# One Strassen pair less in a weight-gradient matmul: 23 instead of 24, with a new order of visits and of the sums between them

## Chip, core and metric

The kernel runs on one core of a Trainium2 chip. The metric is device time in microseconds (us) of one execution. A profiled execution also gives a span: from the first to the last of the program's own instructions.

## What is computed

```python
batch, m, k, n = 16, 512, 1024, 768
input:       (16, 512, 1024) float32
grad_output: (16, 512, 768)  float32
grad_weight = np.einsum('bmk,bmn->kn', input, grad_output).astype(np.float32)
```

Batch and m are summed over together: with X the input as 8192 x 1024 and G the gradient as 8192 x 768, the result is X transposed times G, 1024 x 768.

## The kernel before

**Loads.** The 8192 rows are taken in 32 *pairs* of 256 rows, numbered 0 to 31 here as in `u` of the code. GpSimd's queue loads each of them with a cast from float32 to bfloat16: first G of the pair (line 113), then X (line 114). Only pairs 0 and 1 come in smaller pieces, and the first 128 rows of X and the first of G come in float32 over the queues of ScalarE and SyncE and are rounded on the chip (lines 88 to 91 and 210 to 220). Eight loads can be under way: in the built program each load from the ninth on waits for the one eight places before it, and from the buffers' second use on also for who used the buffer last. 14 pairs of buffers hold the loaded pairs (`PAIRS_HELD`), 9 the sums made from them (`SUMS_HELD`).

**Two kinds of pair.** `LOADS` (line 12) has one letter per pair. A *plain* pair ("s") is two items of 128 rows. X has a left and a right half of 512 columns, G two halves of 384. Each item is multiplied in four blocks A, B, C, D (half of X by half of G), and each block in four parts q of 128 columns of X: 16 matmuls an item, 32 a pair, each of a 128 x 128 weight and 384 columns. A *Strassen* pair ("P") takes its 256 rows as a 2 x 2 block product and forms it with seven products instead of eight: A, D and five more called m, n, o, p, q, each again in four parts: 28 matmuls a pair. For that VectorE makes five sums per pair (`sum_g1`, `sum_g2`, `sum_x1`, `sum_x2`, `sum_x3`, lines 132 to 157): `sum_g1` is the one addition that gives all three block sums of G, because G's column halves are swapped (`LEFT`, `RIGHT`), and `sum_g2` and `sum_x3` work in place. The products o and p need, besides the loaded X, only `sum_g2`; q and n need `sum_x1`; m needs `sum_x2`; A and D need `sum_x3`.

**Visits.** Nine running results A, B, C, D, m, n, o, p, q lie in SBUF in float32 (`acc`, `macc`). PSUM has eight banks, so two of the nine can be open at a time, four banks each: two *slots*. `ORDER` (lines 18 to 32) is written out by hand or by a search; each word is a *visit*. In `1p12:3~!0,0,1,0` the letter is the result, 12 says up to which of its items it goes, and `!` says that the visit closes the slot. To close is to bring the four banks back: by VectorE, which adds the bank to the running result (line 357), or by ScalarE. The number after the colon says for how many banks (the last ones) ScalarE does it: it copies the running result into the bank before the first matmul (`carry`, line 296), TensorE adds on top, and ScalarE copies the bank back (line 353). `^` and `~` let ScalarE fill those banks as soon as the slot's last user has left them, bank by bank (`^`) or when all four have been left (`~`). The digit in front (1 here) says how many entries of the *filler* list VectorE works off before the visit, and the four after `!` how many before each bank is closed. The filler list is the five sums of each Strassen pair in order and then the 20 `SHARES`, which add the five products to A, B, C and D at the end. `A36:0-q` opens A with ScalarE filling its banks with minus q (line 323).

So every engine's order is fixed: TensorE's by `ORDER`; VectorE's and ScalarE's by the closes and fills in it; GpSimd's by the pairs. A matmul waits for its pair to have landed, for the sums that it reads, and for its bank. The last visit is D; its last part is split in two (lines 388 to 402), so that the last stores are short.

Of the kernel before, what the change touches and what calls it, by code (L numbers as in the profile page):

```python
# [8 lines left out]

P = 128  # L10

LOADS = "ssssssPPPPPPPPPPPPPPPPPPPPPPPPss"

ORDER = (
    "A1:4!0,0,0,0 C1:3 B1:2 B2!0,0,0,0 C2!0,0,0,0 A2!0,0,0,0 D3:1 C3:2~ D4!0,0,0,0 C4!0,0,0,0 A4 "
    "B4:2~ A6!0,0,0,0 B6!0,0,0,0 D6!0,0,0,0 C8:3~!0,0,0,0 A8:4~!0,0,0,0 D8:1^!0,0,0,0 B10!0,0,0,0 "  # L20
    "C9 A10:3^!0,0,0,0 C12!0,0,0,1 B12:1~!0,0,0,2 D12:1~ 2A12:4 A13!0,1,2,2 D13 p2:4!0,0,0,0 "
    "n2:3!0,0,1,0 D14!0,0,0,0 m2:4!0,0,1,0 o3:4!3,0,0,0 1A15:1^!0,0,0,4 q3:4 q4!1,0,0,0 1p4:3~ "
    "n4:2!0,0,0,0 p5!1,0,1,0 2m4:2~ D17:2!0,0,0,1 o6:2!1,1,1,0 m6!1,0,0,0 A18:4~!1,0,0,0 4n6:2~ "
    "1n7!0,0,0,0 q7:2~!0,0,0,1 o8!0,1,0,0 3p8:2^ D19:4^ D20!1,1,0,1 p9!0,0,0,0 m9 2A21:4!0,0,3,0 "
    "m10!0,0,0,0 4q9:2~ 2n10:4!0,0,0,0 q11!0,0,3,0 o11:2~ 1p12:3~!0,0,1,0 o12!0,0,0,0 "
    "D24:1~!0,0,4,0 2A24:2~ A25!0,0,0,1 1m13:3^!0,0,0,0 n14!0,1,0,0 q14:4~!0,1,1,4 o15:2~ "
    "1D26:3~!0,2,0,0 o16!0,0,0,1 1m16!1,0,1,0 p16:4^ q17:3^!0,0,0,0 4p17!0,1,0,0 1n17 "
    "1A30:4!0,0,0,0 n18 4n19!1,0,0,1 D30:4^ o18:3~ 2D31!0,1,2,0 o20!1,1,1,0 2m20 m21!0,0,0,0 "
    "q21:3^!2,1,0,3 p19:4^ p20 A32:1^ A34!0,0,0,0 p21 4D34:3~!0,3,0,0 p23 p24!0,0,1,0 "
    "q24:2^!0,0,1,0 m24:3~!0,0,1,1 o24:3~!0,0,1,0 2n22:4~ 1n23 2A36:0-q n24!0,1,0,0 A39 "  # L30
    "B16:4!0,3,1,0 2A40!0,0,0,0 C16:3!0,0,1,1 D40!0,1,1,0 "
).split()


SHARES = (
    "t20 t21 t22 t23 l20 t10 t11 t12 l21 t13 l10 l11 l12 l13 l22 l23 l30 l31 l32 l33 "
).split()

WARMUP = [512] * 10 + [128] * 2
# [7 lines left out]
def kernel(  # L47
# [58 lines left out]
    xg = []  # L106
    for u, kind in enumerate(LOADS):
        pool = pairs if u else head
# [343 lines left out]
```

## Time and profile before

| | |
|---|---|
| median of 3 runs | 164.74 us (164.50 to 164.87) |
| the profiled execution | 164.74 us, its span 163.0 us |
| TensorE clock granted | 1.00 throughout |
| matmuls | 946: 12 of warm-up, 922 of 384 columns, 12 in the split last part |
| ScalarE copies bank to result / result to bank | 154 / 129 (4 of them minus q) |
| VectorE banks closed (the split one counted once) | 118 |
| VectorE sums / shares | 120 / 20 |

All times below that carry no other name are us from the start of the span of this one execution. Lines like L337 are lines of the kernel before. In a timeline row the first number is the start, the second the length from the first start to the last end of the merged instructions, `xN` how many they are, and the bracket how long the engine sat idle before them and what released it. TensorE's matmuls overlap: each row shows one as 0.33 us long, and the next starts before it ends.

### The profile page before, as it was taken

To read this page: it belongs to the slowest core of one execution; us is meant where nothing else is said; L and a number is where in the kernel's file an instruction comes from. 1 tells how busy PE (TensorE), PEld (TensorE's weight loads), DVE (VectorE), ACT (ScalarE), POOL (GpSimd) and SP (SyncE) were. 2 spreads that over 40 slices of the span, in tenths; PEclk is the share of its full clock that TensorE was granted. 3 is DMA by queue.
4 is the path that set the end of the run, shared out by engine and by line. 5 is a ranking of instruction groups with operands and counts; after the bars stand their busy time and mean duration, and the time that the engine had idled before them with its cause. 6 is when DMAs were issued, how large, how long until landed. Compare 5 with 4: busy or idle time off the path is not lost.

```text
span 163.0 us, 2787 instructions
## 1 busy us (share of the span) xinstructions
PE 156.8 (96%) x946; PEld 92.0 (56%) x946; DVE 140.2 (86%) x266; ACT 122.0 (75%) x289; POOL 34.8 (21%) x69
## 2 busy tenths in 40 slices
PE   8899969999999999999999999999999999999992
PEld 3365536666555556666566666555666655655661
DVE  0475845699898999999999999999798979999992
ACT  3875377655988999969987788689767659998830
POOL 7442222212222222222222222122222000000000
PEclk9999999999999999999999999999999999999999
DMA  5999999999999999999999999999999999600595
GB/s 174 297 211 213 215 210 214 214 215 212 212 213 212 213 211 216 212 212 212 213 215 213 214 213 214 214 212 212 210 214 215 211 211 215 135 4 2 197 367 208
DMA packets 12398, 33.40 MB, mean 205 GB/s; under 512 B 1376, under 2 KB 4192, under 8 KB 12384
## 3 DMA queue, kind: packets, MB, share of 16 engines
q0 software_dynamic: 9360, 28.64, 88.8%
q1 hardware_dynamic: 2592, 3.47, 6.1%
q10 hardware_dynamic: 432, 1.11, 1.8%
q8 instruction: 7, 0.11, 0.3%
q14 instruction: 7, 0.06, 0.1%
HBM read 58.72 MB, written 3.15 MB: 380 GB/s over the span
## 4 chain that ended last, share of the span: by engine, by line
PE 67%; DVE 14%; DMA 13%; ACT 2%; issue 2%; DVEq 0%; ACTq 0%; POOLq 0%
PE bank L337 66%; DMA xp<-in_input_dram 9%; DMA gp<-in_grad_output_dram 4%; DVE macc L357 3%; DVE ge L138 2%; DVE xe L148 2%; DVE gp L143 2%; DVE acc L357 2%; DVE xp L157 2%; ACT bank L296 1%; ACT macc L353 1%; DVE xe L152 1%; PE bank L392 0%; DVE acc L400 0%; DVEq L357 0%
## 5 line engine op out<-in xcount | busy, mean ns | idle before, releaser
L337 PEld LDWEIGHTS <-xp 128*128 128x128 bf16 x634 | 61.6, 98 | 44.9 <-DMA xp<-in_input_dram 2.0
L337 PE MATMUL bank<-gp,xp 128*128 128x384 bf16 x444 | 76.8, 326 | 2.1 <-DMA xp<-in_input_dram 1.4
L353 ACT COPY acc<-bank 128x384 f32<-128x384 f32 x71 | 31.1, 491 | 17.4 <-PE bank L337 17.0
L337 PEld LDWEIGHTS <-xe 128*128 128x128 bf16 x288 | 27.9, 98 | 19.5 <-DVE xe L148 0.5
L353 ACT COPY macc<-bank 128x384 f32<-128x384 f32 x83 | 35.4, 503 | 2.5 <-PE bank L337 2.4
L357 DVE TENSOR_TENSOR acc<-bank,acc 128x384 f32<-128x384 f32 x58 | 29.4, 552 | 9.0 <-PE bank L337 8.4
L296 ACT COPY bank<-macc 128x384 f32<-128x384 f32 x64 | 29.4, 501 | 6.7 <-DVE macc L357 4.4
L337 PE MATMUL bank<-ge,xp 128*128 128x384 bf16 x190 | 34.1, 326 | 0.1
L337 PE MATMUL bank<-gp,xe 128*128 128x384 bf16 x192 | 33.7, 326 | 0.0
L296 ACT COPY bank<-acc 128x384 f32<-128x384 f32 x61 | 27.5, 497 | 4.6 <-DVE acc L357 4.2
L357 DVE TENSOR_TENSOR macc<-bank,macc 128x384 f32<-128x384 f32 x52 | 26.5, 552 | 2.0 <-PE bank L337 2.0
L114 POOL DMA_DIRECT2D xp<-in_input_dram x30 | 16.0, 532 | 54.0 <-DMA xp<-in_input_dram 28.1
L113 POOL DMA_DIRECT2D gp<-in_grad_output_dram x30 | 16.0, 533 | 36.3 <-PE bank L337 13.5
L138 DVE TENSOR_TENSOR ge<-gp 128x1152 bf16<-128x1152 bf16 x24 | 18.1, 753 | 0.0
L337 PE MATMUL bank<-ge,xe 128*128 128x384 bf16 x96 | 17.3, 326 | 0.1
L157 DVE TENSOR_TENSOR xp<-xp 128x1024 bf16<-128x1024 bf16 x24 | 16.5, 687 | 0.0
L148 DVE TENSOR_TENSOR xe<-xp 128x1024 bf16<-128x1024 bf16 x24 | 16.4, 685 | 0.0
L194 DVE TENSOR_TENSOR acc<-acc,macc 128x768 f32<-128x768 f32 (+1 forms) x20 | 16.3, 873 | 0.0
L143 DVE TENSOR_TENSOR gp<-gp 128x768 bf16<-128x768 bf16 x24 | 13.3, 555 | 0.5
L152 DVE TENSOR_TENSOR xe<-xp 128x512 bf16<-128x512 bf16 x24 | 10.1, 420 | 0.0
L211 DVE CAST gp<-gf 128x192 bf16<-128x192 f32 (+1 forms) x2 | 0.6, 310 | 5.1 <-DMA gf<-in_grad_output_dram 5.1
L96 PE MATMUL bank<-const-bfloat16-1.0 128*128 128x512 bf16 (+1 forms) x12 | 3.9, 499 | 0.8 <-PEq L436 0.8
(18 smaller groups left out, 17.5 us busy)
## 6 DMA issues: line engine op xcount, KB each, us to landing
xp<-in_input_dram POOLq DMA_DIRECT2D x30, 512.0 KB, 16.8
gp<-in_grad_output_dram POOLq DMA_DIRECT2D x30, 384.0 KB, 16.7
out_dram<-acc SPq DMA_DIRECT2D x15, 192.0 KB, 2.0
xf<-in_input_dram ACTq DMA_DIRECT2D x2, 512.0 KB, 5.0
gp<-in_grad_output_dram POOLq DMA_DIRECT2D x3, 192.0 KB, 6.5
xp<-in_input_dram POOLq DMA_DIRECT2D x2, 256.0 KB, 7.8
gf<-in_grad_output_dram SPq DMA_DIRECT2D x2, 192.0 KB, 4.3
out_dram<-acc SPq DMA_DIRECT2D x1, 128.0 KB, 1.8
```

Of the source, the lines that this page charges most:

```text
L113: nc.gpsimd.dma_start(out=gp, in_=G[rows, :].rearrange("(p m) n -> p m n", m=2))
L114: nc.gpsimd.dma_start(out=xp, in_=X[rows, :].rearrange("(p m) k -> p m k", m=2))
L138: nc.vector.tensor_add(out=ge.rearrange("p a n -> p (a n)"), in0=g[:, 0 : 3 * NH], in1=g[:, NH : 4 * NH])
L143: nc.vector.tensor_sub(out=g[:, 0::3, :], in0=g[:, 0::3, :], in1=g[:, 2:0:-1, :])
L148: nc.vector.tensor_add(out=xe[:, 0:2, :].rearrange("p a k -> p (a k)"), in0=xp[:, 0, :], in1=xp[:, 1, :])
L152: nc.vector.tensor_add(out=extra[i][0][:, 2, :], in0=xp[:, 0, 0:KH], in1=xp[:, 1, KH:K])
L157: nc.vector.tensor_sub(out=x[:, 1:3, :], in0=x[:, 1:3, :], in1=x[:, 0::3, :])
L194: op(out=dst, in0=dst, in1=src)
L296: nc.scalar.copy(out=bank, in_=sum_of(p, q))
L337: nc.tensor.matmul(bank, stat, mov, start=opening and j == 0 and not carried, stop=close and j == len(items_now) - 1, skip_group_check=car ...
L353: nc.scalar.copy(out=dst, in_=bank)
L357: nc.vector.tensor_add(out=dst, in0=bank, in1=dst)
```

## The change

Three lists change and nothing else; every function stays as it is, the one addition for G's block sums and the early fills by ScalarE included.

```diff
-LOADS = "ssssssPPPPPPPPPPPPPPPPPPPPPPPPss"
+LOADS = "sssssssPPPPPPPPPPPPPPPPPPPPPPPss"
...
-    "A1:4!0,0,0,0 C1:3 B1:2 B2!0,0,0,0 C2!0,0,0,0 A2!0,0,0,0 D3:1 C3:2~ D4!0,0,0,0 C4!0,0,0,0 A4 "
-    "B4:2~ A6!0,0,0,0 B6!0,0,0,0 D6!0,0,0,0 C8:3~!0,0,0,0 A8:4~!0,0,0,0 D8:1^!0,0,0,0 B10!0,0,0,0 "
-    "C9 A10:3^!0,0,0,0 C12!0,0,0,1 B12:1~!0,0,0,2 D12:1~ 2A12:4 A13!0,1,2,2 D13 p2:4!0,0,0,0 "
-    "n2:3!0,0,1,0 D14!0,0,0,0 m2:4!0,0,1,0 o3:4!3,0,0,0 1A15:1^!0,0,0,4 q3:4 q4!1,0,0,0 1p4:3~ "
...
-    "D24:1~!0,0,4,0 2A24:2~ A25!0,0,0,1 1m13:3^!0,0,0,0 n14!0,1,0,0 q14:4~!0,1,1,4 o15:2~ "
-    "1D26:3~!0,2,0,0 o16!0,0,0,1 1m16!1,0,1,0 p16:4^ q17:3^!0,0,0,0 4p17!0,1,0,0 1n17 "
...
-    "q24:2^!0,0,1,0 m24:3~!0,0,1,1 o24:3~!0,0,1,0 2n22:4~ 1n23 2A36:0-q n24!0,1,0,0 A39 "
-    "B16:4!0,3,1,0 2A40!0,0,0,0 C16:3!0,0,1,1 D40!0,1,1,0 "
+    "A1:3!0,0,0,0 C1:1 B1:3 B2!0,0,0,0 C2!0,0,0,0 D2:3 A2 D3 A3 D4!0,0,0,0 A4 B4:1^!0,0,0,0 C4 "
+    "C6!0,0,0,0 A6!0,0,0,0 D6:2~!0,0,0,0 B6:3^ C8!0,0,0,0 B8!0,0,0,0 D8:2~!0,0,0,0 A8!0,0,0,0 "
+    "D9:2 B10!0,0,0,0 D10!0,0,0,0 A10 B12:2^!0,0,0,0 A12!0,0,0,0 D12:3 B14!0,0,0,0 D14!0,0,0,0 "
+    "C13:3^ C14!6,0,0,0 A15:1 1o2:4!1,1,1,0 q2:4!0,1,0,1 A16!0,0,0,0 D16:1^ p3:4!2,1,1,0 "
...
+    "2A28:2~!2,0,0,1 q13!0,0,0,0 n15:3~!2,0,1,1 D28:1^!0,0,1,0 o16:2^!0,0,0,0 q16:2~!2,0,0,1 "
+    "m15:3~ 1p17:3^!4,0,1,1 D30!1,0,0,0 m16 m18!0,0,0,0 q18:4~!1,1,0,1 A32 1n19:4^!4,0,1,2 "
+    "o20:1~!0,1,0,0 D34:3^ 4D35!1,0,0,0 A35!1,0,0,0 o22:2^ p21:4 5p23!1,0,1,1 o23!0,0,0,0 q21:2~ "
+    "q23!3,0,0,0 m21:4~ m23!2,1,0,0 n21:4~ A38:0-q n23!5,0,0,1 A40 B18:4!2,1,0,1 A41!0,0,0,0 "
+    "C17:3 C18!1,0,0,0 D41!3,0,0,0 "
...
-    "t20 t21 t22 t23 l20 t10 t11 t12 l21 t13 l10 l11 l12 l13 l22 l23 l30 l31 l32 l33 "
+    "l20 l21 l22 t20 t21 t22 t10 t11 t12 t13 l23 t23 l10 l11 l12 l13 l30 l31 l32 l33 "
```

Pair 6 becomes a plain pair. Read off the lists and the built program:

| | before | after |
|---|---|---|
| plain / Strassen pairs | 8 / 24 | 9 / 23 |
| matmuls of 384 columns, the split part counted as six | 928 | 932 |
| sums on VectorE | 120 | 115 |
| banks closed by VectorE / by ScalarE | 118 / 154 | 124 / 148 |
| banks filled by ScalarE (minus q among them) | 129 | 124 |
| shares, loads, stores | 20, 69, 17 | 20, 69, 17 |

The loads stand in the same order with the same sizes on the same queue.

## The prediction

> **What bounds the kernel now.** First the page's busy times and TensorE's timeline, to see whether its matmuls run back to back.
>
> ```profile
> PE 156.8 (96%) x946; PEld 92.0 (56%) x946; DVE 140.2 (86%) x266; ACT 122.0 (75%) x289; POOL 34.8 (21%) x69
> ```
> ```profile
> 5.18 15.42 PE L337 MATMUL bank<-gp,xp 128*128 128x384 bf16 x90 [0.50 <-DVE xp L211]
> 21.97 16.75 PE L337 MATMUL bank<-gp,xp 128*128 128x384 bf16 x102 [1.37 <-DMA xp<-in_input_dram]
> ...
> 140.62 2.76 PE L337 MATMUL bank<-gp,xp 128*128 128x384 bf16 x16
> 143.22 2.76 PE L337 MATMUL bank<-gp,xe 128*128 128x384 bf16 x16
> ...
> 147.88 7.96 PE L337 MATMUL bank<-gp,xp 128*128 128x384 bf16 x48
> ```
>
> Sixteen matmuls take 143.22 - 140.62 = 2.60 us: 0.1625 us each, the price of a matmul below. I call *delay* the start of the n-th matmul of L337 (from 0) less n x 0.1625. It only grows, and each step in it is a wait. Start: 5.18. Matmul 89 starts one length (0.33) before the first row ends: 20.60 - 0.33 - 14.46 = 5.81. Matmul 90: 21.97 - 14.63 = 7.34. In the row at 147.88 begins matmul 856 (72 follow of 928): 147.88 - 139.10 = 8.78. From there to the end it stays. So TensorE is paced by its own matmuls, 928 x 0.1625 = 150.8, plus three portions of waiting: 0.63 at the start, 1.53 in one piece before matmul 90, and 1.44 in small pieces from there to 147.88.
>
> Second, what the 1.53 waits for: GpSimd's timeline. Each load waits for the one eight places before it, so in this stretch its start tells when that one had landed.
>
> ```profile
> 16.44 0.53 POOL L114 DMA_DIRECT2D xp<-in_input_dram  x1 [1.91 <-DMA xp<-in_input_dram]
> ...
> 22.21 0.53 POOL L114 DMA_DIRECT2D xp<-in_input_dram  x1 [3.38 <-DMA xp<-in_input_dram]
> ...
> 25.90 0.53 POOL L114 DMA_DIRECT2D xp<-in_input_dram  x1 [1.93 <-DMA xp<-in_input_dram]
> ...
> 30.21 0.53 POOL L114 DMA_DIRECT2D xp<-in_input_dram  x1 [1.91 <-DMA xp<-in_input_dram]
> ...
> 34.52 0.53 POOL L114 DMA_DIRECT2D xp<-in_input_dram  x1 [1.93 <-DMA xp<-in_input_dram]
> ```
>
> These are X of pairs 2 to 6 landing: 16.4, at most 22.2 (TensorE goes on at 21.97, so by then), 25.9, 30.2, 34.5. Pair 3 is 1.4 late against the pace of 4.32 a pair. I put pair u at 25.9 + 4.32 x (u - 4).
>
> Third, the small pieces: busy times by stretch, and VectorE at 98 us.
>
> ```profile
> 38.00:102.32 64.32, 64.14 (x392) 37.71 (x390) 62.64 (x122) 55.15 (x134) 15.90 (x30) 1.00 1.07 213
> ```
> ```profile
> 97.50 0.56 DVE L143 TENSOR_TENSOR gp<-gp 128x768 bf16<-128x768 bf16 x1
> 97.97 0.68 DVE L148 TENSOR_TENSOR xe<-xp 128x1024 bf16<-128x1024 bf16 x1
> 98.58 0.42 DVE L152 TENSOR_TENSOR xe<-xp 128x512 bf16<-128x512 bf16 x1
> 98.91 0.69 DVE L157 TENSOR_TENSOR xp<-xp 128x1024 bf16<-128x1024 bf16 x1
> 99.51 0.75 DVE L138 TENSOR_TENSOR ge<-gp 128x1152 bf16<-128x1152 bf16 x1
> 100.30 0.56 DVE L143 TENSOR_TENSOR gp<-gp 128x768 bf16<-128x768 bf16 x1
> ...
> 102.17 1.02 DVE L357 TENSOR_TENSOR macc<-bank,macc 128x384 f32<-128x384 f32 x2
> ```
>
> VectorE (third busy time) works 62.64 of 64.32, as tight as TensorE: whenever a sum or a close stands late in its queue, TensorE waits a tenth or a quarter of a us. From start to start a pair's five sums cost 0.47 + 0.61 + 0.33 + 0.60 + 0.79 = 2.80, and a bank 1.02 - 0.55 = 0.47. On ScalarE four copies back to back took 1.63 us at 5.55 and seven fills 2.96 us at 19.66: (1.63 - 0.48) / 3 = 0.38 and (2.96 - 0.48) / 6 = 0.41.
>
> **The change, part by part.** The sum is made against the span, 163.0; the profiled execution took 164.74, 1.74 more, and the median of the runs is the same 164.74.
>
> *Four matmuls more*: 4 x 0.1625 = **+0.65**, on TensorE's own path, nothing hides it.
>
> *VectorE*: five sums less, 2.80, and six banks more, 6 x 0.47 = 2.82: **0** in all. But it moves. By matmul 592 of the new order the queue holds 77 sums and 90 banks, by matmul 588 of the old one 83 and 90. Six sums, some 3.3 us, come later against the matmuls. If that room is not usable, the cover of the small waits stays as it is.
>
> *ScalarE*: six copies and five fills less, 6 x 0.38 + 5 x 0.41 = 4.3 us. ScalarE is busy 55.15 of 64.32 in the tight stretch, so this shortens no path by itself: **0**, hidden under TensorE.
>
> *The start.* The first 20 matmuls are the same ones; A1 now gives its first bank to VectorE, ahead of the rounding of G's right half: at most 0.1, covered by C1's four matmuls. The new order does B6 (eight matmuls on pair 2) before C8, so pair 3 is first read by matmul 96, not 90. If the delay stays at 5.81, TensorE is there at 5.81 + 15.60 = 21.41, pair 3 at 21.97: the wait shrinks from 1.53 to 0.56, and the delay after it is 21.97 - 15.60 = 6.37 instead of 7.34: **-0.97**. Cover: the fills of B6 and the closes of C6, A6 and D6 must be done by then; at 0.47 and 0.41 apiece they end near 21.0, with half a us in hand. Bounds: -0.97 and 0.
>
> *The next loads* must not take it back. With the delay at 6.37, first reads and landings are: pair 4, matmul 128, 27.2 against 25.9; pair 5, 152, 31.1 against 30.2; pair 6, 176, 35.0 against 34.5; pair 8, 229, 43.6 against 43.2; pair 13, 362, 65.2 against 64.8; pair 22, 602, 104.2 against 103.7; pair 28, 761, 130.0 against 129.6; pair 29, 785, 133.9 against 133.9. All in time, several by only 0.4. Where it fails, TensorE waits, and all later loads have that much more room. Most products also need sums after the landing. The tightest is q on pair 12 (matmul 341, 61.8), which needs `sum_x1`. From pair 10's landing at 51.8 VectorE's queue up to it holds 1.53 of pair 10's sums, 2.80 of pair 11's, 1.26 of pair 12's and seven banks, 3.29: 8.9 us, and it idles some 0.6 for o4's first bank: it comes to `sum_x1` at 61.3 and ends (0.68) at 62.0: 0.2 late.
>
> *The small waits*, 1.44 before, become s. At least 0.2 (pair 12); at most what they were, 1.44, unless something new turns up. VectorE has less in front of it, ScalarE 4.3 us less to do, which speaks for less; the landings are closer, which speaks against. I take **0.8**, the middle, since neither row decides.
>
> *The shares' order, the stores, GpSimd's loads*: the same instructions; the shares stand under the last 100 matmuls, where they stood, the last visit is D with 24 matmuls on a free slot as before, and the stores on SyncE's queue follow the same closes: **0**. If VectorE came late into D41 (three shares stand before its first bank, 1.4 us), the next banks cover it, 0.97 of matmuls for each 0.47.
>
> Sum: 163.0 + 0.65 - 0.97 - 1.44 + 0.8 = 162.04; with 1.74, **163.8**.
>
> [...]
>
> **The rivals.**
>
> *The landings take it back.* For: six of these first reads have 0.5 us or less in hand, and pair 3 shows that a load can be 1.4 late. Against: the other rows keep the pace within 0.05. One later load behind by pair 3's 1.4, with 0.4 in hand, gives 1.0 of wait; with 0.4 of the small waits left beside it s is 1.4: 164.4, at the edge of no change.
>
> *The head doesn't arrive.* The fills of B6 hold TensorE past 21.97, price up to the 0.97: 164.75, no change. For: fills and closes alternate on ScalarE there. Against: half a us in hand.
>
> *Sums in front of the only free slot: slower.* In the new order several sums stand in one heap before a bank that TensorE needs next: four before p17's first bank plus one before the visit, and D30 opens on p17's banks, because m15 holds the other slot. VectorE then has 2.80 + 0.47 = 3.3 us against p17's 2.6 us of matmuls: 0.7 late. The same heaps stand at C14 (6), n19 (5), p23 (6), n23 (5). Every heap at 0.6 makes 3.0 for five: s = 3.0, 166.0. It decides from s = 2.1 (0.65 - 0.97 - 1.44 + s above 0.33, the 0.2% that the measurement can tell). Against: VectorE comes to p17 with fewer sums behind it, and most heaps stand before long visits on the other slot.
>
> **How the numbers follow.** Forecast, s from 0.2 to 1.3, 163.2 to 164.3: 0.62. Landings: 0.14, half of it faster. Head: 0.09, no change. Heaps: 0.15, from 165.1 up. Below 164.41 (0.2% under 164.74): 0.62 + 0.07 = 0.69; within 0.2%: 0.07 + 0.09 = 0.16; slower 0.15. The range goes from 163.2, the forecast's own low end, over landings and head to 164.9.
>
> **What would show it.** In TensorE's timeline after: the run before pair 3 holds 96 matmuls, with an idle of about 0.4 before 21.97; the delay at the last visit is 6.9 to 7.7 instead of 8.78; no idle of over 0.6 after 22 us; 932 matmuls; VectorE's busy time within 1 us of 140.2 and ScalarE's 4 to 6 lower. Wrong would be: a delay above 7.3 at matmul 96, waits of TensorE for X after 22 us that add to over 1, or idle of 0.5 before D30, n19 or p23.

## The result and the profile after

| | before | after |
|---|---|---|
| median | 164.62 us (164.49 to 164.87, 4 runs) | 163.30 us (163.14 to 163.50, 4 runs) |
| span of the profiled execution | 163.0 us | 161.5 us |
| matmuls of 384 columns, the split part as six | 928 | 932 |

The ratio is 0.9918, 95% interval 0.9901 to 0.9936: 1.3 us faster, where 163.8 had been forecast. First the page of the kernel after: busy times, and the head of its chain of waits.

```profile
PE 157.4 (97%) x950; PEld 92.8 (57%) x950; DVE 140.9 (87%) x267; ACT 118.0 (73%) x278; POOL 34.8 (22%) x69
...
PE 84%; DMA 12%; issue 1%; DVE 0%; POOLq 0%
```

The head of the same chain in the kernel before:

```profile
PE 67%; DVE 14%; DMA 13%; ACT 2%; issue 2%; DVEq 0%; ACTq 0%; POOLq 0%
```

VectorE is where it was (140.2 before), ScalarE has 4.0 us less. VectorE and ScalarE, with 14% and 2% of the chain before, have all but gone from it. Next TensorE's timeline of the kernel after: start, length, engine, line, and in the bracket, if any, the idle time.

```profile
5.21 36.66 PE L337 MATMUL bank<-gp,xp 128*128 128x384 bf16 x218
...
146.97 7.35 PE L337 MATMUL bank<-gp,xp 128*128 128x384 bf16 x44
```

The long row of before broke after 90 matmuls, at the wait for pair 3. Here it runs on through 218. There is still a wait in it, too short to break a row in which each matmul counts as 0.33 us: matmul 95 starts at 21.31 and matmul 96, the first to read pair 3, at 21.73, 0.42 later instead of 0.1625. The delays (start of the n-th matmul less n x 0.1625) add it up:

| portion of the delay | before | after | change |
|---|---|---|---|
| up to and with the wait for pair 3 | 7.34 (matmul 90) | 6.13 (matmul 96) | -1.21 |
| small waits from there to the end | 8.78 - 7.34 = 1.44 | 6.61 - 6.13 = 0.48 | -0.96 |
| four matmuls more | | 4 x 0.1625 | +0.65 |
| sum | | | -1.52, the spans (163.0 and 161.5) say -1.5 |

GpSimd's timeline of the kernel after, X of pairs 2, 3 and 4 landing (each load starts when the one eight places before it is in):

```profile
16.45 0.53 POOL L114 DMA_DIRECT2D xp<-in_input_dram  x1 [1.93 <-DMA xp<-in_input_dram]
...
21.97 0.53 POOL L114 DMA_DIRECT2D xp<-in_input_dram  x1 [3.13 <-DMA xp<-in_input_dram]
...
25.95 0.53 POOL L114 DMA_DIRECT2D xp<-in_input_dram  x1 [1.93 <-DMA xp<-in_input_dram]
```

Pair 3 is late here too, by 0.24 less than before. The stretch of the small waits, in the columns us, PE, weight loads, VectorE, ScalarE, GpSimd, granted clock, DMA share, GB/s:

```profile
38.00:102.32 64.32, 64.32 (x396) 38.51 (x395) 61.86 (x119) 55.40 (x133) 15.90 (x30) 1.00 1.07 213
```

TensorE has no idle left and passes 396 matmuls instead of 392; VectorE works 0.78 us less in the same stretch (61.86 for 62.64). That work came earlier: between 21.97 and 38 us VectorE is busy 13.84 us instead of 10.74.

### The profile page after: what moved, and what is told of

It reads as the page before. It is cut to its first block, busy times and chain, and to the rows that moved or that the text cites. A ratio compares the mean times of both kernels' runs of the same rounds, so it can differ in the third digit from the quotient of the medians.

```text
span 161.5 us, 2781 instructions
## 1 busy us (share of the span) xinstructions
PE 157.4 (97%) x950; PEld 92.8 (57%) x950; DVE 140.9 (87%) x267; ACT 118.0 (73%) x278; POOL 34.8 (22%) x69
## 4 chain that ended last, share of the span: by engine, by line
PE 84%; DMA 12%; issue 1%; DVE 0%; POOLq 0%
PE bank L337 84%; DMA xp<-in_input_dram 9%; DMA gp<-in_grad_output_dram 4%; PE bank L392 0%; DVE acc L400 0%; POOLq L436 0%
## 5 line engine op out<-in xcount | busy, mean ns | idle before, releaser
L337 PEld LDWEIGHTS <-xp 128*128 128x128 bf16 x650 | 63.3, 98 | 43.5 <-issue 0.8
L337 PE MATMUL bank<-gp,xp 128*128 128x384 bf16 x468 | 81.1, 327 | 0.1
L353 ACT COPY macc<-bank 128x384 f32<-128x384 f32 x91 | 39.4, 493 | 9.7 <-PE bank L337 9.4
L357 DVE TENSOR_TENSOR acc<-bank,acc 128x384 f32<-128x384 f32 x80 | 39.8, 552 | 5.8 <-PE bank L337 5.5
L353 ACT COPY acc<-bank 128x384 f32<-128x384 f32 x57 | 24.8, 485 | 13.9 <-PE bank L337 13.9
L296 ACT COPY bank<-macc 128x384 f32<-128x384 f32 x73 | 33.0, 496 | 1.6 <-DVE acc L357 0.9
L296 ACT COPY bank<-acc 128x384 f32<-128x384 f32 x47 | 21.6, 494 | 8.9 <-DVE acc L357 7.2
L357 DVE TENSOR_TENSOR macc<-bank,macc 128x384 f32<-128x384 f32 x35 | 18.1, 553 | 1.3 <-PE bank L337 1.3
L337 PE MATMUL bank<-ge,xe 128*128 128x384 bf16 x92 | 15.9, 326 | 0.0
L355 DVE COPY acc<-bank 128x384 f32<-128x384 f32 x6 | 3.2, 555 | 3.3 <-PE bank L337 3.2
```

The lines of the kernel that those rows point to most:

```text
L296: nc.scalar.copy(out=bank, in_=sum_of(p, q))
L337: nc.tensor.matmul(bank, stat, mov, start=opening and j == 0 and not carried, stop=close and j == len(items_now) - 1, skip_group_check=car ...
L353: nc.scalar.copy(out=dst, in_=bank)
L357: nc.vector.tensor_add(out=dst, in0=bank, in1=dst)
```

## The experiments

Times are medians; the kernel before ran beside each group and stood at 164.53 to 164.59 there.

### The early block alone, in the kernel before

```diff
-    "B4:2~ A6!0,0,0,0 B6!0,0,0,0 D6!0,0,0,0 C8:3~!0,0,0,0 A8:4~!0,0,0,0 ...
+    "B4:2~ A6!0,0,0,0 B6!0,0,0,0 D6!0,0,0,0 C6:3~ C8!0,0,0,0 A8:4~!0,0,0,0 ...
```

The 24 pairs and the order stay, but C first takes pair 2, so pair 3 is first read by matmul 96.

> The kernel before with one visit split: C8 becomes C6 and C8, so that eight matmuls on pair 2 come first and pair 3 is first read by matmul 96 instead of 90. Nothing else changes; 24 Strassen pairs, the same 928 matmuls. Theory (the wait for pair 3 is a term of its own): delay after pair 3 about 6.2 to 6.4 instead of 7.34, the later small waits stay about 1.4, time 0.8 to 1.0 us below the kernel before, 163.6 to 163.8. Rival (VectorE, busy 62.6 of 64.3 us, takes it back): the delay at the end is again 8.4 to 8.8, time 164.3 to 164.6.

Measured: 163.65 (163.46 to 163.86, 8 runs), ratio 0.9949 [0.993, 0.9967]. TensorE's timeline of this kernel, a view that ends at some 30 us:

```profile
5.21 16.42 PE L337 MATMUL bank<-gp,xp 128*128 128x384 bf16 x96
21.95 8.30 PE L337 MATMUL bank<-gp,xp 128*128 128x384 bf16 x50 [0.33 <-DMA xp<-in_input_dram]
```

The idle before pair 3 fell from 1.37 to 0.33, the delay after it from 7.34 to 6.35, and it stays: the end's delay is 7.73, so the small waits are 1.38, about as in before (1.44). The wait for pair 3 is a term of its own, and moving its first read is worth 0.94 us alone.

### The kernel after without its early block

```diff
-    "C6!0,0,0,0 A6!0,0,0,0 D6:2~!0,0,0,0 B6:3^ C8!0,0,0,0 B8!0,0,0,0 ...
+    "C6!0,0,0,0 A6!0,0,0,0 D6:2~!0,0,0,0 C8!0,0,0,0 B8:3^!0,0,0,0 ...
```

Pair 3 is first read by matmul 88.

> The changed kernel with the visits B6 and C8 changed about and B6 joined to B8, so that pair 3 is first read by matmul 88 instead of 96; same 932 matmuls, same sums, same closes. Theory: delay after pair 3 about 7.4 instead of 6.13, and the small waits after it stay near 0.5: time 1.1 to 1.3 us above the changed kernel, 164.4 to 164.6. Rival (the waits are one pool, a later start only removes later waits): the delay at the end grows by 0.5 or less, time 163.3 to 163.8.

Measured: 163.42 (163.31 to 163.54, 6 runs), ratio to before 0.9934 [0.9909, 0.996]. The gain did not go, against what I expected. GpSimd's timeline of this kernel tells why (pairs 3 and 4):

```profile
20.73 0.53 POOL L114 DMA_DIRECT2D xp<-in_input_dram  x1 [1.93 <-DMA xp<-in_input_dram]
...
25.90 0.53 POOL L114 DMA_DIRECT2D xp<-in_input_dram  x1 [2.78 <-DMA xp<-in_input_dram]
```

Pair 3 landed on pace; the lateness, the idle of 2.78, went to pair 4, which nobody was waiting for yet. So pair 3 is not late as such: something delays one load, not always the same one.

### What delays the load

A load arrives in 16 parts, and each raises the load's semaphore. In before, 15 parts of pair 3's X were in by 20.48 and the sixteenth at 21.92. The DMA records hold one packet of another kind at that time. The DMA queues from 19.8 to 20.9 us, in before (columns: packets, MB, share of the 16 engines):

```profile
q0 software_dynamic: 84, 0.22, 104.2%
q8 instruction: 1, 0.02, 5.4%
```

One 16 KB packet of the kind *instruction*, called code packet from here on, 0.945 us long from 19.89 on. In before seven such packets come, 19.0 to 23.8 us from one start to the next, and 234 to 277 instructions of TensorE lie between one and the next. That they carry TensorE's own code is my guess from these counts; the records don't name an engine. My second guess was that one sixteenth of the awaited load stands behind the packet. Over all 14 profiles:

| profile | code packet starts | 15 parts of pair 3's X in | the 16th |
|---|---|---|---|
| more sums, before | 19.57 | 20.50 | 21.65 |
| pair count, mended, with early block | 19.62 | 20.45 | 21.66 |
| after | 19.65 | 20.54 | 21.68 |
| pair count, first try, with early block | 19.74 | 20.47 | 21.82 |
| pair count, first try | 19.82 | 20.46 | 21.85 |
| pair count, mended | 19.82 | 20.40 | 21.85 |
| before with early block | 19.88 | 20.55 | 21.91 |
| before | 19.89 | 20.48 | 21.92 |
| before, eight warm-up matmuls | 20.16 | 20.43 | 20.66 |
| more sums, after | 20.21 | 20.41 | 20.55 |
| after, float32 warm-up | 21.01 | 20.44 | 20.45 |
| before, float32 warm-up | 21.98 | 20.43 | 20.43 |
| after without early block, sixteen warm-ups | 23.20 | 20.56 | 20.73 |
| after without early block | 23.28 | 20.41 | 20.44 |

With the packet before 20.0, the last part is 1.1 to 1.5 us behind; with a packet from 20.16 on, at most 0.23. Where the packet comes later, a part of the next loads is late instead, by less (0.86 in after without its early block, 0.80 in before with the float32 warm-up). The runs of before split in the same way: of the 56 beside the experiments 50 took 164.42 to 164.88 and six 163.25 to 163.63, none between.

Can the packet be moved? Two kernels shift TensorE's code by the number of its warm-up matmuls (12 in both kernels; each is a weight load and a matmul).

```diff
-WARMUP = [512] * 10 + [128] * 2
+WARMUP = [512] * 8
```

> Before, with eight warm-up matmuls in place of twelve and nothing else: TensorE's code stands four matmuls (eight instructions) earlier at every point of the real work. In the profiles so far a 16 KB instruction packet of about 0.95 us was moved at 19.9 us by one of the 16 DMA engines (before, one-part experiment of the early block and after: 19.65 to 19.89), and the last of the 16 parts of pair 3's X then landed 1.4 us behind the other fifteen; in the kernel after without its early block, TensorE stood at its wait for pair 3 six to eight matmuls earlier, the packet came at 23.28 and pair 3 landed whole at 20.44. Theory (the code fetch makes pair 3 late, and TensorE's place in its code sets when it comes): TensorE now stops at matmul 90 ahead of the place that asks for the packet, so the packet comes after 20.44, pair 3's X lands whole by 20.4 to 20.5, the wait falls from 1.4 to 1.7 us to under 0.3, and the time falls by 1.0 to 1.3 us, to 163.3 to 163.7. Rival (pair 3 is late for another cause, its place in the line of loads or what the VectorE and ScalarE do then): packet wherever it likes, pair 3's last part still at 21.9, time 164.4 to 164.8. A lower clock in the first matmuls, for want of warm-up, would show as a larger delay at matmul 12 (5.72 before) and add to both.

Measured: 164.62 (163.41 to 165.20, 12 runs), ratio 1.0 [0.9977, 1.0024]. The median was the rival's. But two runs lie at 163.41 and 163.50, and the profiled one is the first: packet at 20.16, pair 3 whole at 20.66, matmul 90 at 20.70 with a delay of 6.08. In that profile the packet comes 0.27 later than in before. That is no more than it differs between kernels whose TensorE code is the same up to there (after 19.65, after with more sums 20.21), so this run doesn't show that eight instructions move it. The first matmuls do run at a lower pace: in before the warm-up matmuls of 512 columns start 0.42 to 0.43 us apart between 1.15 and 3.71 us and 0.22 apart from 3.96 on, and the records of the granted clock begin at 3.77. With eight of them, matmul 12 starts at 7.84 here, a delay of 5.89 for 5.72 in before.

In the second, the kernel after without its early block gets four warm-up matmuls more:

```diff
-WARMUP = [512] * 10 + [128] * 2
+WARMUP = [512] * 8 + [128] * 8
```

> The kernel after without its early block (pair 3 first read by matmul 88, measured 163.42), with sixteen warm-up matmuls in place of twelve (eight of 512 and eight of 128 columns), so that TensorE's code stands four matmuls later at every point of the real work. Theory (code fetch): the place that asks for the 16 KB packet is now passed before the wait at matmul 88, the packet comes at about 19.5 to 20 us as in the kernels before and after, one part of pair 3's X lands at about 21.9, TensorE waits some 1.4 us at matmul 88 and the time is 164.3 to 164.7. Rival (the order without the early block finds pair 3 on pace by itself): 163.3 to 163.6, pair 3 landed by 20.5.

Measured: 163.29 (163.22 to 163.54 and 163.63, and one run of 164.63; 12 runs), ratio to before 0.9936 [0.9916, 0.9957]. My theory missed again: the packet stayed at 23.20. So in this order, where TensorE waits for pair 3 at matmul 88, it is not the count of instructions alone that sets when the packet comes. What does, I don't know.

A larger shift settles the other half. Three float32 warm-up matmuls take the place of the twelve. The expectation below counts them as 3 instructions instead of 24; the trace records 6 matmuls and 6 weight loads, 12 instead of 24, so the shift lies between 12 and 21 instructions:

```diff
-WARMUP = [512] * 10 + [128] * 2
+WARMUP = [512] * 3
...
-    ones = nc.const_aps.tensor(1.0, (P, P), bf16)
+    ones = nc.const_aps.tensor(1.0, (P, P), f32)
...
-            nc.const_aps.tensor(1.0, (P, cols), bf16),
+            nc.const_aps.tensor(1.0, (P, cols), f32),
```

> Before, with the twelve bfloat16 warm-up matmuls replaced by three of float32 (512 columns) and nothing else: 3 instructions in place of 24, so all real code of TensorE stands 21 instructions earlier, some 10 matmuls or 1.7 us of its way. The runs so far fall into two groups 1.1 us apart: of 36 runs of before 33 lie at 164.4 to 164.9 and 3 at 163.3 to 163.6; with eight instructions fewer ahead, 2 of 12 were fast and the one profile of those shows the 16 KB code packet at 20.16, pair 3's X whole at 20.66 and no wait for it, where the slow profiles show the packet at 19.6 to 19.9 and pair 3 whole at 21.7 to 21.9. Theory (the code packet, where it comes before pair 3's X is whole at some 20.5, holds one of its 16 parts back): the packet now comes after 20.6 in nearly all runs, and the median falls into the fast group: 163.3 to 163.8, delay at matmul 90 below 6.4 instead of 7.34. Rival (pair 3's lateness has another cause, and the packet only happens near it): nearly all runs stay at 164.4 to 165. A cold clock in the first matmuls would show by matmul 12 (delay 5.72 before) and add to either.

Measured: 163.82 (163.42 to 164.33, 12 runs), ratio 0.9963 [0.9941, 0.9985]; all 12 are below the 164.42 where the larger group of before begins. The DMA queues of this kernel from 19.8 to 20.9 us and from 21.9 to 23 us:

```profile
q0 software_dynamic: 85, 0.23, 104.7%
```
```profile
q0 software_dynamic: 58, 0.23, 102.3%
q8 instruction: 1, 0.02, 5.4%
```

No code packet in the first stretch, where before had it. Pair 3 in GpSimd's timeline, and TensorE's start (a view from 4 us to some 30, so the first row holds only the last three of the six warm-up records):

```profile
20.72 0.53 POOL L114 DMA_DIRECT2D xp<-in_input_dram  x1 [1.93 <-DMA xp<-in_input_dram]
```
```profile
3.47 2.77 PE L96 MATMUL bank<-const-float32-1.0 128*128 128x512 f32 x3
6.03 24.15 PE L337 MATMUL bank<-gp,xp 128*128 128x384 bf16 x144
```

Pair 3 is on pace and TensorE doesn't stop for it: 144 matmuls without a break up to the end of the view. The expectation of a delay below 6.4 at matmul 90 missed (6.61), because the longer warm-up lets the first real matmul start at 6.03 instead of 5.18; less this 0.85 it is 5.76. The small waits are 1.40, as in before. So a code packet ahead of the landing is what makes pair 3 late, and moving it away takes the wait of 1.4 away, in the kernel before, with its order untouched.

The same warm-up in the kernel after:

> After, with the same three float32 warm-up matmuls. Theory (code packet): the packet comes after pair 3 is whole, the 0.42 us gap before matmul 96 goes, and the delay at matmul 96 falls from 6.13 to 5.85 or so: 163.0 to 163.2, so that after gains at most 0.3 where before gains 1.1; the two kernels then stand within 0.6 us of each other. Rival: unchanged at 163.1 to 163.5 with the wait at matmul 96 still there.

Measured: 163.24 (162.91 to 163.77, 9 runs), ratio to before 0.9936 [0.9914, 0.9957]. Its profile (packet at 21.01, pair 3 whole at 20.45, delay at matmul 96 5.82, first matmul at 5.47) is the expected one, but belongs to the fastest run, 162.91. The median doesn't tell it from after's 163.30. Nothing that ran is clearly faster than after.

### The pair count alone

Four kernels took one pair out of the order of before: `LOADS` as after, every product's item number one lower, a plain item more in A, B, C and D.

```diff
-    ... 2A12:4 A13!0,1,2,2 D13 p2:4!0,0,0,0 n2:3!0,0,1,0 D14!0,0,0,0 m2:4!0,0,1,0 o3:4!3,0,0,0 ...
+    ... A12:4 A14!0,0,0,0 D14 B14:1!0,0,0,0 C14!0,1,2,2 p1:4!0,0,0,0 n1:3!0,0,1,0 D15!0,0,0,0 m1:4!0,0,1,0 o2:4!3,0,0,0 ...
```

> The kernel before with pair 6 made plain and its order else kept word for word (all items counted on by the pair, B14 and C14 put in behind A14 and D14, the ten sums before them cut to five): the number of pairs alone. Matmuls +4, 0.65. Rival one (the sums taken from VectorE's queue are what removes the small waits): they fall from 1.44 to about 0.5, time 164.2 to 164.5. Rival two (the searched order does it, the count nothing): they stay at 1.3 to 1.5, time 165.1 to 165.4. The wait for pair 3 stays whole in both, delay 7.3 to 7.4 after it.

> Both edits of the two kernels on the old order: pair 6 plain, and C8 split so that pair 3 is first read by matmul 96. If the terms add up, it is the sum of the two: with rival one (count) 163.2 to 163.6, level with the changed kernel; with rival two (order) 164.1 to 164.4.

Measured: 171.31 (ratio 1.0428 [1.0398, 1.0458]), and with the early block 170.43 (1.0364). Both missed by 6 us. Some visits had shrunk to four matmuls, which I took to be too short for a bank to be turned over beside them. The mended pair drops those visits:

```diff
-    ... 2A12:4 A13!0,1,2,2 D13 p2:4!0,0,0,0 n2:3!0,0,1,0 D14!0,0,0,0 m2:4!0,0,1,0 o3:4!3,0,0,0 ...
+    ... A12:4 A14!0,0,0,0 D14 B14:1!0,0,0,0 C14!0,1,2,2 D15!0,1,1,0 o2:4!3,0,0,0 ...
```

> The pair count alone, in the order of before: 23 Strassen pairs, one pair less, in place of which two row blocks go the plain way (four more matmuls, +0.65 us), without the single-item visits that stalled the first try. Theory one (the small waits of before, 1.4 us, come from VectorE's sums being too many, so one pair less takes them away): 164.2 to 164.5, delay gained after the wait for pair 3 about 0.5. Theory two (the small waits come from the order of visits, so that the pair count alone only costs its matmuls): 165.1 to 165.4, delay gained after pair 3 about 1.3 to 1.5.

> The kernel of the run of the pair count alone, with the early visit of the third block split as in the run of the early block alone (which took 0.94 us off before), so that pair 3 is first read later. Theory one (sums): 163.2 to 163.6, as fast as after, and the order of the visits further on is worth nothing. Theory two (order): 164.1 to 164.4, and the 0.8 to 1.0 us that after is faster than this is the order's.

Measured: 172.55 (1.0496 [1.0462, 1.053]) and 171.64 (1.0438 [1.0405, 1.0472]). Missed as well, and 1.2 us slower than the first try, so the short visits were not what cost the 6 us. What the trace shows is that in the queue of VectorE the first sums now stand behind closes that come late, and that it sits idle for 6.17 us before 41.6, waiting for TensorE. TensorE's timeline of the mended kernel without the early block, and its busy times by stretch (the columns as above):

```profile
47.22 1.46 PE L325 MATMUL bank<-ge,xp 128*128 128x384 bf16 x4 [3.26 <-DVE xp L145]
...
49.96 2.40 PE L325 MATMUL bank<-gp,xp 128*128 128x384 bf16 x7 [0.97 <-DVE gp L131]
```
```profile
47.20:50.00 2.80, 1.82 (x6) 0.77 (x7) 2.67 (x6) 0.96 (x2) 1.02 (x2) 0.50 1.08 216
50.00:54.00 4.00, 4.00 (x14) 1.92 (x14) 3.39 (x7) 1.92 (x4) 0.70 (x3) 0.53 1.08 215
54.00:58.00 4.00, 3.81 (x24) 2.09 (x23) 3.96 (x8) 2.11 (x5) 0.93 (x2) 1.00 1.07 212
```

A wait of 3.26 us, and after it the granted clock is at 0.50 for some 6.6 us: 14 matmuls in 4 us instead of 24. These four runs don't answer the question that they were made for. What they show is that the list of a pair can't be taken out of a hand-fitted order alone: the places of the sums between the visits belong to it. The early block took 0.9 off both times here too.

### VectorE's room

`sum_x2` is done twice in ten Strassen pairs.

```diff
+        first = LOADS.index("P") * 2
+        for _ in range(2 if 2 <= i - first < 12 else 1):
-        nc.vector.tensor_add(out=extra[i][0][:, 2, :], in0=xp[:, 0, 0:KH], in1=xp[:, 1, KH:K])
+            nc.vector.tensor_add(out=extra[i][0][:, 2, :], in0=xp[:, 0, 0:KH], in1=xp[:, 1, KH:K])
```

> After, with sum_x2 done twice in ten Strassen pairs (the third to the twelfth): 10 x 0.33 = 3.3 us more on VectorE between some 47 and 86 us, a little more than the five sums of one pair (2.80 in the prediction); nothing else changes and the result is the same. VectorE is busy 61.86 of 64.32 between 38 and 102.3 in after. Theory one (the order of visits is what made the small waits small: VectorE's room is usable there): small waits rise from 0.48 to between 0.5 and 1.3, time +0.1 to +0.9, 163.4 to 164.2. Theory two (the removed sums were the cover: one pair's sums put back bring the small waits back and more): +1.0 to +2.5, 164.3 to 165.8.

> Before, with the same ten additions done twice in its third to twelfth Strassen pairs: VectorE is busy 62.64 of 64.32 in that stretch, 1.68 idle. Both theories: at least 3.3 - 1.7 = 1.6 us more waiting, 166.2 to 168. If it rises by less than 1, VectorE's fullness was not what the small waits of before come from.

Measured: in after 166.21 (165.96 to 166.58), 2.9 more than after; in before 168.02 (167.9 to 168.13; 1.0224 [1.0194, 1.0255]), 3.5 more than before. The second lies at the upper end of what was expected, 168. The first lies above both theories: of 3.3 us more on VectorE, 2.9 arrive at the end. The stretch of 64.32 us again, after and then before, each with the added sums:

```profile
38.00:102.32 64.32, 62.33 (x378) 36.13 (x377) 62.44 (x123) 52.98 (x126) 15.90 (x30) 1.00 1.07 213
```
```profile
38.00:102.32 64.32, 62.52 (x372) 35.43 (x371) 62.98 (x125) 53.59 (x130) 15.90 (x30) 1.00 1.07 213
```

VectorE gains hardly 0.6 of busy time and TensorE loses 18 matmuls (396 to 378): the idle time of VectorE in after, 64.32 - 61.86 = 2.46, is not room. Of it 1.1 us are waits of a sum for its load and 1.0 of a close for its matmuls; with the added sums the 1.1 is still there. In after, too, VectorE is as near to the bound as TensorE; the profile without added work doesn't show it, because there no matmul behind pair 3 is held up by VectorE. With the added sums 2.94 us of late starts have VectorE as the last engine waited for, in before 3.48. My theory one, that the new order leaves VectorE room, is refuted. In before, 1 us of it costs 1.05, in after 0.88.

## Why the prediction was right

*Four matmuls*, +0.65: exact.

*The start*, -0.97: measured -1.21. The mechanism is shown by the early block alone (0.94 us). The term was undersized because the landing of pair 3 was taken over from before, 21.97; in the execution after, the code packet began 0.24 earlier and so did the landing. The gap before matmul 96 is 0.42 from start to start, 0.26 of it wait; forecast was 0.56 of wait. The first three gaps between matmuls are about 0.3 in after and give away 0.43; before loses about as much at matmuls 10 to 12, and at matmul 12 the delay is 5.72 in both.

What the prediction had not seen is what the wait was made of: it took pair 3's lateness for a fact of the loads. It is one part of a load behind a code packet, and by the run times it is there in 50 of 56 runs of before. Where it isn't, before takes 163.4 (the middle of six runs), and after's measured 163.3, in whose profiled run pair 3 was late, is hardly better. So of the 1.3 us some 0.9 to 1.0 are cover against that packet; the rest is 0.96 less of small waits against 0.65 of matmuls. That the size came out near the forecast is in part luck: pair 3's load was late in both profiled runs, and the prediction didn't know that it can be on time. The two terms that were off, 0.24 at the start and 0.32 in the small waits, add up to the 0.5 us by which the forecast was high.

*The small waits*, s = 0.8: measured 0.48. This is the term that was mis-sized most; I had taken the middle of 0.2 and 1.44 for want of a row that decides. It is not an accident of one profile: in the four profiles of before's order with neither pairs nor sums changed the small waits are 1.38 to 1.44, in the four of after's order 0.36 to 0.53.

The prediction put them down to VectorE's queue, and ScalarE at 0, "hidden under TensorE". The traces say otherwise for the larger part. They hold the semaphores that each matmul waits for; the one raised last tells which engine a late matmul waited for. In before it is ScalarE for 0.92 us of the small waits and VectorE for 0.49; in after ScalarE for 0.47 and VectorE for none (the rest is too small to place). Two places in the chain of before, each ending at a late matmul (number 298 at 56.20, 0.23 late; number 578 at 102.32, 0.25 late):

```profile
54.59 1.17 ACT macc L353 x3
55.76 0.39 ACT bank L296
56.15 0.04 issue
56.20 2.11 PE bank L337 x12
...
101.33 0.60 DVE xe L148
101.92 0.35 DVE xe L152
102.27 0.05 issue
102.32 56.45 PE bank L337 x344
```

The first stands behind ScalarE's copies and a fill, the second behind VectorE's sums. What ScalarE and VectorE had waited for themselves at the other late matmuls was not followed. So the fall of 0.96 is about half ScalarE's (0.45) and half VectorE's (0.49). The 0.78 us of VectorE's work that left the tight stretch would be enough for its half, at 0.88 to 1.05 us of waiting for each; that this is the cause is argued. For ScalarE's half no run was made. Whether the missing pair or the places of the visits and sums bring either stays open, since the four runs on the pair count failed.

*VectorE 0, ScalarE hidden*: the busy times went from 140.2 to 140.9 and from 122.0 to 118.0, as said; that ScalarE's 4.0 us are worth nothing is not what the waits show. *The next loads*: TensorE shows no wait for X after 22 us, though from pair 4 to pair 6 one part of each load of X is 0.83 to 0.88 late in the records (25.67 for pair 4, whose first read is at 26.94). *Pair 12's q*, forecast as the tightest, 0.2 late: matmul 341 shows no step (under 0.01). With the added sums this place opens, by 0.62, after 0.39 at matmul 322.

*The rivals*: landings and heaps did not come; at D30, n19 and p23 no idle shows. The head arrived. *Which engine binds*: by its matmuls' own pace TensorE is taken for 150.8 of 163.0 us, 93%, which is above VectorE's 86%. The added sums show that VectorE binds as well as soon as it gets more work: of 3.3 us more on it 2.9 arrive at the end in after, and in before the time grows by 3.5.

*The signs to look for*: 96 matmuls before pair 3, 932 in all, no idle of 0.6 after 22 us: all there. The delay at the end, 6.61, lies below the 6.9 to 7.7 that I had named, by the two terms above.

## What to carry to other kernels

A load that is late once and then never again deserves a look at the packets of other kinds in that microsecond, and at the spread of the runs: two groups a fixed distance apart can mean, as here, that one event falls now before, now after a landing. Give the first read of such a load other work on TensorE to stand behind where the order allows it: here eight matmuls cost nothing and took 0.94 of the 1.4 us. Before an engine is put down as hidden, look which semaphore the late matmuls waited for last. And before calling an engine's idle time room, add work to it: 2.5 us of idle in a 64 us stretch took up only 0.4 of 3.3.

## What the hardware showed unexpectedly

A code packet of 16 KB (0.89 to 0.95 us at its first coming) held back one part of a load here. Where the first one started before 20.0 us, the part of pair 3's X landed 1.1 to 1.5 us late, and one part stayed some 0.5 to 1.0 late in the next loads, which follow each other without a gap. The six later packets of each run are of the same size, but no part of a load near them is over 0.8 us late, and most are under 0.5; why the first costs more was not tried.

The granted clock fell after less than a full pause. In the first try of the pair count no idle of TensorE was longer than 1.25 us, but from 44.0 to 47.7 it ran only three matmuls. Its busy times (matmuls, then the clock) from 49 to 50 and from 53 to 54 us:

```profile
49.00:50.00 1.00, 1.00 (x5) 0.50 1.01 205
...
53.00:54.00 1.00, 1.00 (x9) 1.00 1.03 209
```

Half the clock from about 49 to 52.4, some 1.7 us lost on top of the waits. In the mended kernel, by the clock's records, the fall came at 46.9 us, 2.9 us after the end of the last matmul (43.96). The clock came back after 3.4 us in the first try, but only after 6.7 us (53.8) in the mended kernel. In the first try a sparse stretch of 3.7 us, without a full pause, came ahead of the fall; how short or how sparse it may be was not tried. In before, the wait of 1.4 us at pair 3, with full work on either side, left the clock at 1.00.
